# The MLP's second product turned to rows of tokens, 21 of its 32 groups computed with seven block products

## The chip, the cores and the metric

The kernel runs on one core of a Trainium2 chip. A core has TensorE (PE, with its weight loads shown apart as PEld), VectorE (DVE), ScalarE (ACT), GpSimd (POOL) and SyncE (SP), whose queue here issues nearly all DMAs. Each engine executes its own instructions in a fixed order and waits on semaphores for the others. The metric is the device time of one execution in microseconds (us). Before the change it was 2890.46 us, the median of three runs (2887.89 to 2895.62).

## The reference

One encoder layer over 2048 tokens of width 1024, in float32. The part that the change touches is the last one:

```python
h = h + xo @ w_xo[l]                         # after cross-attention
u = rmsnorm(h, norm_mlp_g[l]) @ w_up[l]      # 1024 -> 4096
h = h + jnp.square(jax.nn.relu(u)) @ w_down[l]   # 4096 -> 1024
return rmsnorm(h, norm_final_g)
```

Before it come a mixing layer (dilated sliding-window attention with three patterns, beside a width-31 convolution) and cross-attention to 256 memory tokens.

## The kernel before

**Numbers.** Every large product keeps float32 accuracy by splitting each operand in a high part (rounded by a cast) and a low part (the remainder). `mm3` (L198 to L201) then issues three matmuls: high by high, low by high, high by low. `wsplit2` (L187 to L192) makes the two parts of a weight tile: an ACT cast for the high part (L190), a subtraction for the low part (L191), on VectorE unless another engine is named.

**Stages.** A first part prepares the memory, the projections and the attention of the first tokens. Then four passes `post(p)`, p = 0 to 3, each take 512 tokens through the output projection (tiles `o`), cross-attention (`xs`, `x`), the MLP (`up`, `dn`) and the final norm. Beside the MLP of passes 0, 1 and 2 run the windowed attention and the convolution of the next 512 tokens: `weave` advances these generators by 0.95 and 0.6 of a step for each step of the pass. Pass 3 has nothing beside it. A scheduler then places every engine's instructions, so neighbouring steps interleave.

**The MLP of one pass.** The hidden 4096 features are cut in eight groups `fg` of 512. A group first makes its hidden values: four times 24 matmuls (`up`, 8 chunks of the contraction by 3), each into one of three PSUM banks; `rl` is max(0, up) times the norm's scale (VectorE, L1321), squared on ScalarE (L1322), and split in `hhh` (ACT, L1323) and `hhl` (VectorE, L1324). Then it multiplies by its 512 rows of `w_down`: for each of eight blocks of 128 output features, 12 matmuls (4 chunks by 3) with the weight as the stationary operand and 512 tokens as the moving one (`dn`), and VectorE adds the bank to `h` (L1339). `h` has features on partitions. After the last group `final` squares and sums over partitions, transposes each block of `h` by TensorE (`ot`, L1367), scales and stores.

**The feed of weights.** Each group loads eight tiles of 512 KB (four `raw_u`, four `raw_d`) through `wpost`: a DMA on SP into one of two `raw` buffers, ACT cast, VectorE subtraction, into one of four pairs `whi`/`wlo`. A `raw` buffer is free again after its subtraction, a pair after its last matmul. Each tile serves 24 matmuls.

**GpSimd** serves the attention beside the MLP: casts of queries (L821), the merging of the attention patterns (L914 to L939) and low parts in the convolution's norm (L272).

## Time and profile before

| | us |
|---|---|
| median of three runs | 2890.46 |
| the profiled execution | 2888.26 |
| its span, first to last instruction | 2886.5 |
| PE busy in the span | 2826.6 |
| VectorE busy | 1857.6 |
| ScalarE busy | 1166.3 |
| GpSimd busy | 458.0 |
| mean granted TensorE clock | 0.994 |

In the span, pass 0's MLP runs from 892 to 1287 us, pass 1's from 1442 to 1834, pass 2's from 1989 to 2380, and pass 3's from 2521 to the end. A row of groups reads: line, engine, operation, output<-inputs, shape and count, then busy time and mean duration of one, then the engine's idle time before these instructions and what ended it. A row of windows reads: the stretch, its length, busy time and count for PE, PEld, DVE, ACT and POOL, then the granted clock, the DMA engines' share and GB/s. Matmuls overlap one another, so the spacing of matmuls, and not the mean duration in a row, is what one of them costs.

### The profile page before, as it was taken

The numbers are of one execution on the slowest core, as the hardware profiler recorded it, in microseconds if no ns is written. First come the engines' busy times: TensorE is split into PE (matmuls) and PEld (weight loads), VectorE is DVE, ScalarE is ACT, GpSimd is POOL, SyncE is SP. The second block draws the span as 40 slices with busy tenths as digits, with TensorE's granted clock in tenths as the row PEclk, the third lists the DMA queues.
The fourth block names the chain that finished last, engine by engine and source line by source line (L and its number), as shares of the span: only waits on it lengthen the run. The fifth ranks groups of instructions, "written<-read, shape, count | busy, mean of one in ns | idle before, by whom it ended". The sixth has DMA issues, their size and how long they took to land.

```text
span 2886.5 us, 41313 instructions
## 1 busy us (share of the span) xinstructions
PE 2826.6 (98%) x15628; PEld 2376.2 (82%) x15628; DVE 1857.6 (64%) x3306; ACT 1166.3 (40%) x1988; POOL 458.0 (16%) x469
## 2 busy tenths in 40 slices
PE   8999999998999999999999999999999999999999
PEld 7878899887788888888888888888888888888887
DVE  5636535565789776557887765689876555544445
ACT  5633211475554333434543343444333433432233
POOL 1336421122102011200012012002011200000000
PEclk9999999999999999999999999999999999999999
DMA  8979845799734444554444446534543445333332
GB/s 264 295 173 228 202 132 131 182 256 247 205 102 131 135 133 123 168 160 145 121 130 130 138 117 192 175 96 128 142 127 109 139 132 175 93 90 101 96 95 74
DMA packets 598632, 433.74 MB, mean 150 GB/s; under 512 B 191550, under 2 KB 524786, under 8 KB 597921
## 3 DMA queue, kind: packets, MB, share of 16 engines
q1 hardware_dynamic: 558256, 408.21, 50.2%
q10 hardware_dynamic: 37952, 16.88, 2.4%
q0 software_dynamic: 2224, 6.01, 0.6%
q8 instruction: 123, 2.02, 0.3%
q14 instruction: 77, 0.62, 0.1%
HBM read 339.89 MB, written 91.11 MB: 149 GB/s over the span
## 4 chain that ended last, share of the span: by engine, by line
PE 82%; DVE 9%; DMA 5%; issue 2%; ACT 2%; POOL 1%; SPq 1%; POOLq 0%; DVEq 0%; ACTq 0%
PE dn L199 8%; PE dn L200 8%; PE dn L201 8%; PE up L199 7%; PE up L200 7%; PE up L201 7%; PE lin L199 4%; PE lin L201 4%; PE lin L200 4%; DVE cacc L216 3%; PE o L199 2%; PE o L200 2%; PE o L201 2%; PE xs L199 2%; PE xs L201 2%; PE xs L200 2%
## 5 line engine op out<-in xcount | busy, mean ns | idle before, releaser
L199 PE MATMUL dn<-hhh,whi_d 128*128 128x512 f32 (+1 forms) x1056 | 402.8, 392 | 7.2 <-DVE h L1339 6.1
L200 PE MATMUL dn<-hhl,whi_d 128*128 128x512 f32 (+1 forms) x1056 | 403.4, 385 | 1.1 <-DVE hhl L1324 1.1
L199 PE MATMUL up<-mh,whi_u 128*128 128x512 f32 x1024 | 402.9, 393 | 0.5 <-DVE rl L1321 0.5
L201 PE MATMUL dn<-hhh,wlo_d 128*128 128x512 f32 (+1 forms) x1056 | 402.6, 384 | 0.0
L200 PE MATMUL up<-ml,whi_u 128*128 128x512 f32 x1024 | 399.4, 390 | 1.0 <-DVE ml L1214 0.9
L201 PE MATMUL up<-mh,wlo_u 128*128 128x512 f32 x1024 | 399.7, 391 | 0.0
L216 DVE SCALAR_TENSOR_TENSOR cacc<-cu,cw,cacc 128x512 f32<-128x512 f32 x480 | 389.0, 811 | 5.5
L190 ACT CAST whi_d<-raw_d 128x1024 fp32r<-128x1024 f32 x128 | 134.6, 1052 | 418.1 <-PE up L200 378.6
L1339 DVE TENSOR_TENSOR h<-h,dn 128x512 f32<-128x512 f32 (+1 forms) x264 | 172.3, 667 | 162.9 <-PE dn L201 161.7
L190 ACT CAST whi_u<-raw_u 128x1024 fp32r<-128x1024 f32 x128 | 134.4, 1050 | 327.2 <-PE dn L200 304.1
L1321 DVE SCALAR_TENSOR_TENSOR rl<-up,ssumx 128x512 f32<-128x512 f32 x128 | 88.0, 690 | 256.9 <-PE up L201 252.6
L199 PEld LDWEIGHTS dn<-hhh,whi_d 128*128 128x128 f32 x1056 | 198.1, 189 | 47.5 <-DVE h L1339 10.2
L201 PEld LDWEIGHTS dn<-hhh,wlo_d 128*128 128x128 f32 x1056 | 198.8, 188 | 39.7
L200 PEld LDWEIGHTS dn<-hhl,whi_d 128*128 128x128 f32 x1056 | 199.3, 189 | 37.4 <-DVE hhl L1324 2.0
L200 PEld LDWEIGHTS up<-ml,whi_u 128*128 128x128 f32 x1024 | 192.4, 188 | 40.1 <-DVE ml L1214 2.3
L201 PEld LDWEIGHTS up<-mh,wlo_u 128*128 128x128 f32 x1024 | 192.2, 188 | 40.3
L199 PEld LDWEIGHTS up<-mh,whi_u 128*128 128x128 f32 x1024 | 192.4, 188 | 38.5 <-DVE rl L1321 0.9
L774 ACT ACTIVATE sm<-sm,o 128x256 f32<-128x256 f32 (+1 forms) x384 | 160.1, 466 | 126.3 <-DVE o L773 125.9
L773 DVE CUSTOM_DVE_ANT_0 sm<-s,mask 128x256 f32<-128x256 f32 (+1 forms) x384 | 128.5, 375 | 83.5 <-PE s L999 39.4
L191 DVE TENSOR_TENSOR wlo_u<-raw_u,whi_u 128x1024 fp32r<-128x1024 f32 x128 | 158.4, 1237 | 32.7 <-ACT whi_u L190 32.4
L191 DVE TENSOR_TENSOR wlo_d<-raw_d,whi_d 128x1024 fp32r<-128x1024 f32 x128 | 163.2, 1275 | 23.8 <-ACT whi_d L190 23.7
L177 POOL TENSOR_TENSOR nr<-st_v,mhalf 128x4 f32<-128x4 f32 (+1 forms) x13 | 13.0, 997 | 839.2 <-DVE st_v L173 839.2
(403 smaller groups left out, 6320.9 us busy)
## 6 DMA issues: line engine op xcount, KB each, us to landing
raw_u<-in_w_up_dram SPq DMA_DIRECT2D x128, 512.0 KB
raw_d<-in_w_down_dram SPq DMA_DIRECT2D x128, 512.0 KB
raw_o<-in_w_out_dram SPq DMA_DIRECT2D x32, 512.0 KB
raw_a<-ascr SPq DMA_DIRECT2D x32, 512.0 KB
raw_b<-bscr SPq DMA_DIRECT2D x32, 512.0 KB
k<-kscr SPq DMA_DIRECT2D x24, 512.0 KB
k<-kscr SPq DMA_DIRECT2D x8, 1152.0 KB
xn<-in_x_dram SPq DMA_DIRECT2D x32, 256.0 KB
```

The source lines that it names most:

```text
L177: POOL.tensor_tensor(dst, v, mhalf.to_broadcast([P, v.shape[1]]), op=ALU.pow)
L190: ACT.copy(hi, raw)
L191: (lo_eng or DVE).tensor_tensor(lo, raw, f(hi), op=ALU.subtract)
L199: PE.matmul(o, lh, rh, start=first, stop=False)
L200: PE.matmul(o, lh, rl, start=False, stop=False)
L201: last["pe"] = PE.matmul(o, ll, rh, start=False, stop=end)
L216: DVE.scalar_tensor_tensor(acc, u[:, t:t + 512], cw[:, c, t:t + 1], acc, op0=ALU.mult, op1=ALU.add)
L773: last["dve"] = DVE.tensor_tensor_reduce(dst, so, mask[:, 256 * m:256 * m + nk], 1.0, 3e38, ALU.add, ALU.min, mn)
L774: last["act"] = ACT.activation(dst, dst, AF.Exp, bias=mn, scale=-1.0)
L1321: last["dve"] = DVE.scalar_tensor_tensor(r, pt, 0.0, rsb, op0=ALU.max, op1=ALU.mult)
L1339: last["dve"] = DVE.tensor_tensor(hs[m][:, sl], hs[m][:, sl], pt, op=ALU.add)
```

## The change

The second product is computed with tokens on the output's partitions: the hidden values become the stationary operand (128 tokens at a time) and 512 columns of `w_down` the moving one. The running sum is kept in `rows` tiles (128 tokens by 512 features). It starts as `h`, transposed by TensorE in the middle of group 0's first product (`to_rows`: 32 transposes and 8 ACT copies a pass), and `final` now works on rows: squares with a sum along the row on ScalarE, one scaling instruction on VectorE for 128 tokens, a store of 512 KB, with no transposes.

In passes 1 to 3, groups 0 to 6 (21 of the 32) use Winograd's form of Strassen's algorithm (`seven`): tokens, hidden features and output features are each cut in two, and seven products of 12 matmuls replace eight. The sums of hidden values (S1 to S4) are built each time, by GpSimd and VectorE (`parts`), and split like the plain ones. The sums of weights are built once, in pass 0, by GpSimd (`sums_of`: four subtractions of 128x256 for each of 28 tiles), written to `dscr` in DRAM by 112 DMAs of 128 KB on SP, and read again in passes 1 to 3. Such a group loads seven tiles of `w_down` kind (three direct, four from `dscr`), each serving 12 matmuls; the low parts of five of the seven are made by GpSimd, of two by VectorE. The running products share PSUM: one pair of banks is added to the rows four times, with further matmuls accumulated between (`more`), another twice, the third once, which makes 14 additions a group in place of 8. Group 7 of each pass, and all of pass 0, keep eight products (`plain`).

The up and down products now rotate over four PSUM banks; the attention beside them has one score bank in place of two during the MLP. The activations' buffers become five interchangeable units of two tiles (`unit`), whose roles rotate from pass to pass.

```diff
@@ -117,6 +117,7 @@
+    dscr = dr.tile([7, 4, P, 2, 512], F32, name="dscr")
@@ -195,10 +196,11 @@
-    def mm3(o, lh, ll, rh, rl, first, end):
-        PE.matmul(o, lh, rh, start=first, stop=False)
-        PE.matmul(o, lh, rl, start=False, stop=False)
-        last["pe"] = PE.matmul(o, ll, rh, start=False, stop=end)
+    def mm3(o, lh, ll, rh, rl, first, end, more=False):
+        PE.matmul(o, lh, rh, start=first, stop=False, skip_group_check=more)
+        PE.matmul(o, lh, rl, start=False, stop=False, skip_group_check=more)
+        last["pe"] = PE.matmul(o, ll, rh, start=False, stop=end, skip_group_check=more)
@@ -1140,20 +1142,19 @@
-    xp_ = pool("post_x")
-    zp = pool("post_z")
-    yp = pool("post_y")
+    un = pool("post_u")
+    role = {x: i for i, x in enumerate("abcde")}
+    def unit(x, name, dtype=F32R):
+        return [un.tile([P, 4, 512], dtype, tag=f"un{role[x]}{i}", name=f"{name}{i}") for i in range(2)]
...
     def load_cat(p, half):
         d = cats.setdefault(p, {})
+        t = unit("ab"[half], f"cat{p}{half}")
         for q in "hl":
-            t = xquad(q, half, f"cat{q}{p}{half}")
             for e in range(4):
-                d[q, 4 * (1 - half) + e] = t[:, e]
+                d[q, 4 * (1 - half) + e] = t["hl".index(q)][:, e]
         for j in range(2):
             load_pair(p, half, j)
...
-        hs = [zp.tile([P, 512], F32, tag=f"z{m}", name=f"h{p}_{m}") for m in range(KC)]
-
-        def ytiles(name):
-            return {(q, k): ytile(q, k, f"{name}{q}{p}_{k}") for k in range(KC) for q in "hl"}
+        else:
+            banks["S"] = (3, 4)
+        he = unit("e", f"h{p}", F32)
+        hs = [he[m // 4][:, m % 4] for m in range(KC)]
+        yt = {q: unit(x, f"y{q}{p}") for q, x in zip("hl", "cd")}
+        y = {(q, k): yt[q][k // 4][:, k % 4] for k in range(KC) for q in "hl"}
...
@@ -1306,80 +1307,204 @@
-        for fg in range(FG):
-            hh = {}
...
+        banks["S"] = (4,)
+        acc = unit("b", f"rows{p}", F32)
+        def row(g, n=1):
+            r = acc[g // 4][:, g % 4:g % 4 + n]
+            return r if n > 1 else r[:, 0]
+        def to_rows(g):
+            t, c = divmod(g, 2)
+            pt = ps("T", f"hT{p}{g}")
+            for i in range(4):
+                PE.transpose(pt[:, P * i:P * i + P], hs[4 * c + i][:, P * t:P * t + P], ident)
+            ACT.copy(row(g), pt)
+        def add_rows(g, pt):
+            last["dve"] = DVE.tensor_tensor(row(g), row(g), pt, op=ALU.add)
+        def split(t, src):
+            ACT.copy(t[0], src)
+            DVE.tensor_tensor(t[1], src, f(t[0]), op=ALU.subtract)
+        def hidden(fg, c, up):
+            wh, wl = wpost(wcols(w_up, fg * 512 + c * P), f"u{p}{fg}_{c}")
+            pt = ps(up, "up")
+            for k in range(KC):
+                mm3(pt, wh[:, k, :], wl[:, k, :], y["h", k], y["l", k], k == 0, k == KC - 1)
+                if fg == 0 and k in ((1, 4) if c == 3 else (3, 7)):
+                    g = 2 * c + (k > 3)
+                    to_rows(2 * (g % 4) + g // 4)
+            r = tmp("rl")
+            last["dve"] = DVE.scalar_tensor_tensor(r, pt, 0.0, rsb, op0=ALU.max, op1=ALU.mult)
+            ACT.activation(r, r, AF.Square)
+            return r
+        def plain(fg, banks_, dn):
+            hh = unit("e" if fg == FG - 1 else "a", f"hh{p}{fg}")
-                wh, wl = wpost(wcols(w_up, fg * 512 + c * P), f"u{p}{fg}_{c}")
-                pt = ps("mm", "up")
...
-                last["dve"] = DVE.scalar_tensor_tensor(r, pt, 0.0, rsb, op0=ALU.max, op1=ALU.mult)
-                ACT.activation(r, r, AF.Square)
-                ACT.copy(hh["h", c], r)
-                DVE.tensor_tensor(hh["l", c], r, f(hh["h", c]), op=ALU.subtract)
+                r = hidden(fg, c, banks_)
+                split([t[:, c] for t in hh], r)
                 yield
             if fg == FG - 1:
-                fsum = ssum_tile(f"f{p}")
                 if not end:
                     load_cat(p + 1, 0)
-            def down(mp2, t, w, wh, wl):
...
+                gr = un.tile([P, 4, 512], F32, tag=f"un{role['d']}0", name=f"gain{p}")
+                gain_row[0] = gr[:, 0:2]
+                dma(gain_row[0].rearrange("p a m -> p (a m)"), A["norm_final_g"].unsqueeze(0).to_broadcast([P, D]))
+                if end:
...
+                        final(2 * th, 2)
...
+            for c in range(2):
+                pts = [ps(dn, "dn") for _ in range(4)]
+                for j in range(2):
+                    raw = wp.tile([P, 2, 2, 256], F32, tag="raw", name=f"raw_d{p}{fg}{c}{j}", bufs=2)
+                    for z in range(2):
+                        dma(raw[:, z], w_down.rearrange("(k p) (h m) -> p k h m", p=P, h=2)
+                            [:, 4 * fg + 2 * z + j, :, 256 * c:256 * c + 256])
+                    n = turn_w[0]
+                    turn_w[0] += 1
+                    wh, wl = wsplit2(wq if n % 4 > 1 else wp, raw, f"d{p}{fg}_{c}{j}", shape=(P, 2, 2, 256))
+                    if p == 0 and fg < FG - 1:
+                        sums_of(fg, c, j, raw)
+                    for t in range(4):
+                        for z in range(2):
+                            mm3(pts[t], *(x[:, 2 * z + j, P * t:P * t + P] for x in hh),
+                                *(x[:, z].rearrange("p h m -> p (h m)") for x in (wh, wl)), j + z == 0, j + z == 2)
+                        if j:
+                            a = row(2 * t, 2)[:, :, 256 * c:256 * c + 256]
+                            last["dve"] = DVE.tensor_tensor(a, a, pts[t].rearrange("p (h m) -> p h m", h=2), op=ALU.add)
+                    yield
+        def sums_of(fg, c, j, raw):
+            n = turn_s[0] % 2
+            turn_s[0] += 1
+            t = wsum[0][:, 2 * n:2 * n + 2].rearrange("p a (s m) -> p (a s) m", s=2)
+            for i, (a, b) in enumerate(((raw[:, 0, 1], raw[:, 0, 0]), (raw[:, 1, 1], t[:, 0]),
+                                        (raw[:, 1, 1], raw[:, 0, 1]), (raw[:, 1, 0], t[:, 1]))):
+                POOL.tensor_tensor(t[:, i], a, b, op=ALU.subtract)
+            for i in range(4):
+                dma(dscr[fg, i, :, j, 256 * c:256 * c + 256], t[:, i])
+        def seven(fg, up):
+            dx, dy = ("ux", "uy") if up == "up" else ("uy", "ux")
+            q = hq
+            A1, S3 = ([x[0][:, s].rearrange("p (j t) -> p j t", j=2) for x in q] for s in (0, 1))
+            A2, S12 = [x[0][:, 2:4] for x in q], [x[1][:, 0:2] for x in q]
+            S4 = [x[1][:, 2].rearrange("p (j t) -> p j t", j=2) for x in q]
+            rs_ = []
+            def parts(c):
+                r, j = rs_[c], c % 2
+                lo, hi = r[:, 0:256], r[:, 256:512]
+                if c < 2:
+                    split([x[:, j] for x in A1], lo)
+                    POOL.tensor_tensor(lo, lo, hi, op=ALU.subtract)
+                    split([x[:, j] for x in S3], lo)
+                else:
+                    r0 = rs_[j]
+                    W = DVE if j else POOL
+                    split([x[:, j] for x in A2], r)
+                    W.tensor_tensor(r0[:, 0:256], hi, r0[:, 0:256], op=ALU.subtract)
+                    W.tensor_tensor(r0[:, 256:512], r0[:, 256:512], hi, op=ALU.add)
+                    split([x[:, j] for x in S12], r0)
+                    W.tensor_tensor(lo, lo, r0[:, 0:256], op=ALU.subtract)
+                    split([x[:, j] for x in S4], lo)
+            for c in range(4):
+                rs_.append(hidden(fg, c, up))
+                for x in ((c - 1, c) if c % 2 else ()) if fg == 0 else (c,):
+                    parts(x)
                 yield
-        def final(t, w):
-            r = rstd_from(fsum[:, t:t + w])
...
-                    dma(out[0, 512 * p + c0:512 * p + c0 + P, 512 * g:512 * (g + 1)], ot)
+            def direct(a, b):
+            half = {"A11": A1, "S3": S3, "S4": S4, "A12": [x[:, :, lo] for x in A2], "A22": [x[:, :, hi] for x in A2],
+                    "S2": [x[:, :, lo] for x in S12], "S1": [x[:, :, hi] for x in S12]}
+            X, Y = ([ps(kind, "dn") for _ in range(2)] for kind in (dx, dy))
+            Z = None
+            for n, (key, w, out_, more, t0, c0) in enumerate((
+                    ("A11", direct(0, 0), 0, False, 0, 0), ("A12", direct(1, 0), 1, False, 0, 0),
+                    ("S2", dscr[fg, 1], 0, True, 0, 1), ("S1", dscr[fg, 0], 2, False, 2, 1),
+                    ("S3", dscr[fg, 2], 0, True, 2, 1), ("S4", direct(1, 1), 2, True, 0, 1),
+                    ("A22", dscr[fg, 3], 0, True, 2, 0))):
+                raw = wp.tile([P, 2, 512], F32, tag="raw", name=f"raw_d{p}{fg}{n}", bufs=2)
+                dma(raw, w)
+                wh, wl = wsplit2(wq if tw % 4 > 1 else wp, raw, f"d{p}{fg}_{n}", shape=(P, 2, 512),
+                                 lo_eng=None if n in (0, 4) else POOL)
+                if out_ == 2 and Z is None:
+                    Z = [ps(dy, "dn") for _ in range(2)]
+                pts = (X, Y, Z)[out_]
+                order_ = [(t, j) for j in range(2) for t in range(2)] if n in (1, 2) else \
+                    [(t, j) for t in range(2) for j in range(2)]
+                for t, j in order_:
+                    mm3(pts[t], *(x[:, j, P * t:P * t + P] for x in half[key]), wh[:, j], wl[:, j],
+                        not more and j == 0, j == 1, more)
+                    if j:
+                        add_rows(2 * (t0 + t) + c0, pts[t])
+                if n % 2 or n == 6:
+                    yield
+        fin = top.tile([P, 8], F32, tag="fin", name=f"fin{p}")
+        def final(t0, n):
+            for g in range(2 * t0, 2 * t0 + 2 * n):
+                ACT.activation(tmp("sq"), row(g), AF.Square, accum_out=fin[:, g:g + 1])
+            fv = fin[:, 2 * t0:2 * t0 + 2 * n].rearrange("p (t c) -> p t c", c=2)
+            sq = top.tile([P, 4], F32, tag="fsq", name="fsq")
+            DVE.tensor_tensor(sq[:, 0:n], fv[:, :, 0], fv[:, :, 1], op=ALU.add)
+            r = top.tile([P, 8], F32, tag="nr", name="nr", bufs=2)
+            rstd_col(r[:, 0:n], sq[:, 0:n], n, top)
+            for t in range(n):
+                x = row(2 * (t0 + t), 2)
+                DVE.scalar_tensor_tensor(x, x, r[:, t:t + 1], gain_row[0], op0=ALU.mult, op1=ALU.mult)
+                dma(out[0, 512 * p + P * (t0 + t):512 * p + P * (t0 + t + 1), :], x.rearrange("p a m -> p (a m)"))
+        banks.update(up=(0, 1, 2, 3), pu=(2, 3, 0, 1), ux=(0, 1), uy=(2, 3), q=(0, 1, 2, 3))
+        turn_s, wsum, hq = [0], [None], []
+        for k in ("up", "pu", "ux", "uy", "q"):
...
+        for fg in range(FG):
+            if fg == 0 and p:
+                hq += [unit("a", f"hh{p}"), unit("e", f"hl{p}")]
+            elif fg == 0:
+                wsum[0] = unit("e", "wsum", F32)[0]
+            if p == 0 or fg == FG - 1:
+                yield from plain(fg, *(("q", "q") if p == 0 else ("pu", "pu")))
+            else:
+                yield from seven(fg, ("up", "pu")[fg % 2])
+            if fg == FG - 1 and not end:
+                role.update(zip("abcde", [role[x] for x in "acdeb"]))
+                load_cat(p + 1, 1)
+        if not end:
+            final(0, 4)
+            for _ in range(4):
```

76 lines of the change are left out of this document (21 added, 55 removed).

## The prediction

> **What bounds the kernel now.** I read the page's first and fourth parts, then windows over the MLP's groups, then groups of instructions by shape inside one pass.
>
> ```profile
> span 2886.5 us, 41313 instructions
> PE 2826.6 (98%) x15628; PEld 2376.2 (82%) x15628; DVE 1857.6 (64%) x3306; ACT 1166.3 (40%) x1988; POOL 458.0 (16%) x469
> PE 82%; DVE 9%; DMA 5%; issue 2%; ACT 2%; POOL 1%; SPq 1%; POOLq 0%; DVEq 0%; ACTq 0%
> PE dn L199 8%; PE dn L200 8%; PE dn L201 8%; PE up L199 7%; PE up L200 7%; PE up L201 7%; PE lin L199 4%; PE lin L201 4%; PE lin L200 4%; DVE cacc L216 3%; PE o L199 2%; PE o L200 2%; PE o L201 2%; PE xs L199 2%; PE xs L201 2%; PE xs L200 2%
> ```
>
> TensorE carries 82% of the chain that ends last, and the two MLP products are 45% of it (24 for `dn`, 21 for `up`). So a matmul removed there is worth its spacing, as long as the other engines follow. Whether they do is read by stage. The rows are: groups 0 to 3 of passes 0, 1 and 2 (of pass 1 also group 0 alone, and groups 4 to 6); one group of pass 3; the time after the last product.
>
> ```profile
> 892.40:1098.90 206.50, 202.93 (x1103) 167.18 (x1102) 166.64 (x274) 77.27 (x124) 33.83 (x33) 0.99 0.47 133
> 1442.40:1645.60 203.20, 200.94 (x1103) 166.20 (x1102) 164.33 (x274) 77.09 (x124) 32.37 (x33) 1.00 0.48 133
> 1442.40:1495.30 52.90, 51.94 (x290) 42.68 (x289) 47.33 (x81) 21.08 (x35) 14.10 (x15) 1.00 0.47 135
> 1645.60:1789.70 144.10, 143.88 (x739) 119.17 (x739) 85.81 (x137) 59.36 (x87) 32.47 (x33) 1.00 0.50 144
> 1988.80:2193.60 204.80, 201.30 (x1100) 165.96 (x1099) 166.38 (x274) 76.95 (x124) 33.82 (x33) 1.00 0.47 131
> 2566.60:2610.20 43.60, 43.60 (x193) 35.91 (x192) 20.41 (x24) 13.04 (x16) 0.00 (x0) 1.00 0.33 96
> 2876.10:2886.50 10.40, 3.44 (x22) 2.48 (x21) 3.58 (x10) 1.79 (x3) 0.70 (x1) 0.75 0.34 132
> ```
>
> PE is never idle for long. VectorE is busy 81% of groups 0 to 3 of pass 1 (164.3 of 203.2), where attention and convolution run beside the MLP, 60% in groups 4 to 6, and 47% in pass 3 (20.4 of 43.6). GpSimd has room everywhere.
>
> **The matmuls removed.** A group of 192 matmuls takes 43.6 us in pass 3: 0.2271 us each at a granted clock of 1.00. A seven-product group has 84 matmuls for 96, so 12 x 0.2271 = 2.73 us less; 21 groups give 57.2 us. The 32 transposes of each pass move from its end into group 0: 0.
>
> **VectorE's part.** Rows of VectorE in pass 1, then in pass 3, then GpSimd, ScalarE, and `cacc` over the whole run (minimum/median/maximum, ns):
>
> ```profile
> L216 DVE SCALAR_TENSOR_TENSOR cacc<-cu,cw,cacc 128x512 f32<-128x512 f32 x78 | 61.2, 785 | 0.7
> L1339 DVE TENSOR_TENSOR h<-h,dn 128x512 f32<-128x512 f32 x63 | 42.1, 681 | 24.0 <-PE dn L201 23.7
> L191 DVE TENSOR_TENSOR wlo_d<-raw_d,whi_d 128x1024 fp32r<-128x1024 f32 x32 | 41.3, 1290 | 5.1 <-ACT whi_d L190 5.1
> L191 DVE TENSOR_TENSOR wlo_u<-raw_u,whi_u 128x1024 fp32r<-128x1024 f32 x30 | 37.5, 1250 | 12.0 <-ACT whi_u L190 11.9
> L1324 DVE TENSOR_TENSOR hhl<-rl,hhh 128x512 fp32r<-128x512 f32 x32 | 24.0, 753 | 0.8 <-ACT hhh L1323 0.5
> ```
> ```profile
> L191 DVE TENSOR_TENSOR wlo_d<-raw_d,whi_d 128x1024 fp32r<-128x1024 f32 x32 | 39.2, 1225 | 11.2 <-ACT whi_d L190 11.2
> L191 DVE TENSOR_TENSOR wlo_u<-raw_u,whi_u 128x1024 fp32r<-128x1024 f32 x29 | 35.5, 1224 | 3.8 <-ACT whi_u L190 3.8
> L1324 DVE TENSOR_TENSOR hhl<-rl,hhh 128x512 fp32r<-128x512 f32 x32 | 22.1, 692 | 0.2 <-ACT hhh L1323 0.2
> L1339 DVE TENSOR_TENSOR h<-h,dn 128x256 f32<-128x256 f32 x6 | 2.3, 419 | 1.2 <-PE dn L201 1.1
> ```
> ```profile
> L191 POOL TENSOR_TENSOR wlo_g<-raw_g,whi_g 128x1024 fp32r<-128x1024 f32 x8 | 19.1, 2394 | 13.9 <-ACT whi_g L190 13.9
> L821 POOL CAST qt<-qh 128x512 fp32r<-128x512 f32 x24 | 29.2, 1217 | 603.3 <-PE s L999 555.5 <-DMA ld<-oscr 47.8
> L529 POOL TENSOR_TENSOR vsq<-vsq 128x256 f32<-128x256 f32 x4 | 3.3, 823 | 0.2
> L190 ACT CAST whi_d<-raw_d 128x1024 fp32r<-128x1024 f32 x128 | 134.6, 1052 | 418.1 <-PE up L200 378.6 <-issue 23.1 <-DMA raw_d<-in_w_down_dram 13.0
> L216 DVE SCALAR_TENSOR_TENSOR cacc<-cu,cw,cacc x480: 698/748/2764, 239.5 to 2186.1; 128x512 f32<-128x512 f32 x160
> ```
>
> Per seven-product group: two `wlo_d` fewer, -2.5 us; 14 additions for 8, +6 x 0.68 = 4.1; the low parts of the hidden values are four of 512 and six of 256 columns for four of 512, +6 x 0.42 = 2.5; three sums of 256 on VectorE, 1.3. Together +5.4 us. GpSimd gains five subtractions of 1024 (12.0) and five of 256 (4.1): 16.1 us, with 8 us of its own in 51, so it isn't full. ScalarE gains three casts (3.2) and narrower splits; at 77 of 203 us it has the room.
>
> GpSimd's work also slows VectorE. Operations with both inputs in SBUF are longer in pass 1 than in pass 3: 32 x 0.065 (`wlo_d`) + 30 x 0.026 + 32 x 0.061 (`hhl`) + 78 x 0.037 (`cacc` against its median) = 7.8 us, for 64.8 us of GpSimd (32.4 and 32.5 in the two rows of windows): 0.12 us for each. This is the low end. At the high end such an operation waits for the whole GpSimd operation it meets (the longest `cacc` took 2.76 us), and with about half of VectorE's time in such operations that is 0.5. I take 0.2, nearer to the measured end, but above it because a 2.39 us subtraction meets more than one operation: 3.2 us a group.
>
> Groups 0 to 3 of pass 1 then ask 164.3 + 4 x (5.4 + 3.2) = 198.7 us of VectorE. PE would need 203.2 - 4 x 2.73 = 192.3. Filled to at most 96%, VectorE takes 207, some 15 us more than PE. A lag of about 5 us can be carried on, since tiles are made ahead, and is worked off in groups 4 to 6 (85.8 + 3 x 8.6 = 112 of 136 us). So PE waits about 10 us in each of passes 1 and 2: 20 in all. That is, the gain of these eight groups (21.8 us) is nearly lost.
>
> **Short waits.** A bank pair is accumulated on again 2.73 us after its last matmul, and between VectorE must add it (0.68 us); before, three banks gave 5.4 us. While PE waits there, the attention's matmuls wait behind. Bounds are 0 (pass 3 now has no idle time) and one addition at each of three reuses, 2.1 us a group. I take 0.6 in pass 3 (VectorE then 28.5 of 40.9 us) and 0.7 in groups 4 to 6: 4 + 4 us. The single score bank is freed by two VectorE operations of 256 columns (0.42) and used again two steps of 24 matmuls later, some 11 us: 0, at most 3.
>
> **Feed.** A load issued at 2563.67 us moves nothing for 1 us, 238 GB/s x 2.2 us (its 512 KB), then nothing:
>
> ```profile
> 2563.67 16.69 SPq L57 DMA_DIRECT2D raw_d<-in_w_down_dram  x4
> ...
> 2563.70:2564.70 1.00, 1.00 (x6) 0.84 (x5) 0.42 (x1) 0.00 (x0) 0.00 (x0) 1.00 0.00 0
> 2564.70:2566.90 2.20, 2.20 (x11) 1.81 (x11) 0.27 (x1) 0.13 (x1) 0.00 (x0) 1.00 0.74 238
> 2566.90:2569.10 2.20, 2.20 (x12) 1.81 (x11) 1.92 (x2) 0.92 (x1) 0.00 (x0) 1.00 0.00 0
> ```
>
> A `raw` buffer's turn is 3.2 + 1.05 + 2.39 + some 0.35 between engines = 7.0 us with GpSimd, 5.8 with VectorE. Eleven tiles over two buffers: (5 x 7.0 + 6 x 5.8) / 2 = 35 us a group, against 40.9 of PE. It is hidden, with 1.0 us to spare a turn (7.4 less 6.4). If GpSimd is late, the next load on SP is late, and with it the loads queued behind. I take 0 beyond the waits above.
>
> **Pass 0.** 112 subtractions by 0.82 us are 92 us of GpSimd, 13 a group, and their 112 stores (14.7 MB) pass through SP ahead of later loads. A `raw` buffer is then held for four subtractions (3.3 us), a turn of 7.8 us where two tiles last 10.9: hidden. VectorE loses 13 x 0.2 = 2.6 us a group, which matters only where it is fullest: +2 us, between 0 and 6.
>
> **The end.** After the last product now 10.4 us. Then: an addition 0.7, a square about as long, the root with GpSimd (0.70) and small steps some 1.9, two scalings of 1024 columns by 1.23, a store of 512 KB 3.2, an estimate of 9 to 9.5: -1, between -3 and +2.
>
> **Sum.** -57.2 + 20 + 4 + 4 + 2 - 1 = -28. Against the profiled execution (2888.26 us) that is 2860; the median shown is 2.2 us above it: about 2863 us.
>
> **The rivals.** *All hidden.* If VectorE keeps up (collisions at 0.12, lag carried), 10 us of waits remain: 2890 - 57 + 5 = 2838. For it: in group 0 of pass 1 VectorE was busy 47.3 of 52.9 us (89%) and PE idle only 1.0. Against it: 198.7 us do not fit in 192.3.
>
> *GpSimd shuts VectorE out* (the slower side). At 0.5 for each microsecond, 8 us a group: groups 0 to 3 ask 164.3 + 4 x 13.4 = 218, at 96% 227, less 192.3 and 5: 30 us in each of two passes. Groups 4 to 6, now 126 of 136 us full, lose 2 each (12), pass 3 1 a group (7), pass 0 4: -57 + 60 + 12 + 7 + 4 = +26, 2916 us. It decides from about 0.4, where the loss passes 57. The longest `cacc` speaks for it, the mean of 0.12 against it. The Trainium skill, page "SBUF — State Buffer", section Terms, says that VectorE and GpSimd share a port pair taken by lock for a whole instruction, so that "the loser **fully blocks**"; by that rule this rival is the case, and the `hhl` row (753 against 692 ns) shows only that operations met seldom so far.
>
> *The feed binds.* If a GpSimd subtraction waits in its queue behind attention work, so that a turn takes 8.4 us for 6.4, a group needs 46 us. This costs 5 us in pass 3 and in groups 5 and 6 of passes 1 and 2 (11 groups, 55 us), nothing where PE needs 47 anyway: 2890 - 57 + 55 = 2888, no change. The `qt` casts, each after some 23 us of waiting for PE (555.5 over 24), speak for it; the 1 us to spare speaks against it.
>
> **Chances.** Likeliest 0.45, its own range 2848 to 2882 (collisions 0.12 to 0.35); all hidden 0.15; shut out 0.20; feed 0.15; others, slower, 0.05. No change means within 0.3%, 2881.8 to 2899.1, about what a measurement of this kernel can tell. Faster: 0.43 + 0.15 + 0.04 of the feed's = 0.62; same: 0.02 + 0.09 = 0.11; slower: 0.20 + 0.02 + 0.05 = 0.27. The range 2836 to 2916 runs from all hidden to shut out and leaves out under 2 in 10.
>
> **What would show it.** Right: 84 `dn` matmuls in each of 21 groups; pass 3's groups at 41 to 42 us; groups 0 to 3 of passes 1 and 2 no shorter than 200 us, VectorE over 93% busy there, PE's waits on additions, `rl` and low parts. Shut out: `wlo_u` and `hl` much longer than 1.22 and 0.69 us wherever GpSimd is busy. Feed: PE waiting for `wlo_d` made by GpSimd, casts waiting for DMAs, in pass 3 too. The prediction fails if pass 3's groups aren't shorter, or if passes 1 and 2 gain as much as pass 3.

## The result and the profile after

The changed kernel takes 3010.97 us (median of four runs, 3009.01 to 3016.3), the kernel before beside it 2890.93: a ratio of 1.0416, with a 95% interval of 1.0402 to 1.043. It is 120 us slower, where the prediction had 2863 us and a range up to 2916. The profiled execution took 3009.49 us, with a span of 3007.7.

First the page of the changed kernel: its span, busy times, and the chain of work that ended last, by engine and by line.

```profile
span 3007.7 us, 41954 instructions
...
PE 2834.0 (94%) x15248; PEld 2338.4 (78%) x15248; DVE 2061.6 (69%) x3501; ACT 1283.2 (43%) x2217; POOL 918.2 (31%) x791
...
PE 55%; DVE 18%; DMA 12%; issue 5%; POOL 5%; ACT 3%; SPq 1%; POOLq 0%; DVEq 0%; ACTq 0%
```

TensorE's share of the chain has fallen from 82 to 55%; VectorE's has doubled, and DMA and GpSimd have more than doubled. GpSimd's busy time has doubled too (458 to 918 us). TensorE issues fewer matmuls and is busy a little longer.

Windows by stage (the stretch, its length, then the busy time of PE, PEld, DVE, ACT and POOL with their counts, the granted clock, the DMA share, GB/s): groups 0 to 3 of pass 0, groups 0 to 3 and 4 to 7 of pass 1, groups 0 to 3 of pass 2, and groups 1 to 6 of pass 3.

```profile
907.10:1124.60 217.50, 209.12 (x1134) 171.67 (x1134) 175.57 (x270) 80.56 (x131) 98.93 (x97) 0.98 0.55 160
1478.20:1723.80 245.60, 215.74 (x1128) 171.61 (x1126) 215.31 (x334) 104.69 (x172) 104.67 (x73) 0.92 0.47 134
1723.80:1920.50 196.70, 183.62 (x839) 146.63 (x839) 127.96 (x176) 87.15 (x127) 76.28 (x61) 0.97 0.58 171
2073.20:2315.90 242.70, 210.86 (x1128) 167.67 (x1126) 217.09 (x332) 103.95 (x172) 106.16 (x73) 0.94 0.46 133
2690.90:2953.20 262.30, 252.51 (x1081) 201.22 (x1080) 171.75 (x223) 110.25 (x151) 96.77 (x60) 1.00 0.43 132
```

Groups 0 to 3 of pass 1 take 245.6 us where they took 203.2; VectorE is busy 215.3 us of these (88%), and TensorE is idle 30 us. In pass 3 six groups take 262.3 us, 43.7 each, as before: with 12 matmuls less in each group, TensorE is now idle 10 us there, though VectorE is busy only 65% of the time and GpSimd 37%.

The time of each stage, from the first `up` matmul of a pass to the next pass's first `o` matmul (us, profiled executions):

| stage | before | after | difference |
|---|---|---|---|
| up to pass 0's MLP | 892.4 | 907.1 | +14.7 |
| MLP of pass 0 | 394.7 | 417.9 | +23.2 |
| MLP of pass 1 | 391.5 | 442.3 | +50.8 |
| MLP of pass 2 | 390.9 | 429.2 | +38.3 |
| MLP of pass 3 and the end | 365.8 | 368.0 | +2.2 |
| what lies between | 451.2 | 443.2 | -8.0 |

Groups of VectorE's instructions in the MLP of pass 1 (line, engine, operation, output and inputs, shape, count, then busy us, mean ns of one, idle time before them):

```profile
L218 DVE SCALAR_TENSOR_TENSOR cacc<-cu,cw,cacc 128x512 f32<-128x512 f32 x74 | 72.7, 984 | 0.5
L1326 DVE TENSOR_TENSOR rows<-rows,dn 128x512 f32<-128x512 f32 x98 | 64.4, 679 | 8.9 <-PE dn L203 8.8
L192 DVE TENSOR_TENSOR wlo_u<-raw_u,whi_u 128x1024 fp32r<-128x1024 f32 x30 | 37.9, 1262 | 33.5 <-ACT whi_u L191 32.7 <-POOL csm L927 0.7
L1331 DVE TENSOR_TENSOR hl<-rl,hh 128x256 fp32r<-128x256 f32 x42 | 35.1, 841 | 10.5 <-ACT hh L1330 10.0 <-PE hT L1322 0.5
L1331 DVE TENSOR_TENSOR hl<-rl,hh 128x512 fp32r<-128x512 f32 x28 | 29.6, 1059 | 7.1 <-ACT hh L1330 7.1
L192 DVE TENSOR_TENSOR wlo_d<-raw_d,whi_d 128x1024 fp32r<-128x1024 f32 x18 | 26.8, 1491 | 10.0 <-ACT whi_d L191 10.0
```

The operations that read both inputs from SBUF are stretched: `cacc` 984 ns (785 before), low parts of 512 hidden values 1059 (753 before), of 256 columns 841 (486 in a kernel without GpSimd work in the seven products, below), `wlo_d` 1491 (1290 before). `rows`, which adds a product out of PSUM, keeps its 679 ns (681 before). `wlo_u` is the exception: it reads both inputs from SBUF and hardly changes (1262, 1250 before).

### The profile page after: what moved, and what is told of

Same layout as the page of the kernel before. It is cut to its first block, busy times and chain, and to the rows that moved or that the text cites. A ratio compares the mean times of both kernels' runs of the same rounds, so it can differ in the third digit from the quotient of the medians.

```text
span 3007.7 us, 41954 instructions
## 1 busy us (share of the span) xinstructions
PE 2834.0 (94%) x15248; PEld 2338.4 (78%) x15248; DVE 2061.6 (69%) x3501; ACT 1283.2 (43%) x2217; POOL 918.2 (31%) x791
## 4 chain that ended last, share of the span: by engine, by line
PE 55%; DVE 18%; DMA 12%; issue 5%; POOL 5%; ACT 3%; SPq 1%; POOLq 0%; DVEq 0%; ACTq 0%
DVE cacc L218 4%; PE lin L201 4%; DMA raw_u<-in_w_up_dram 4%; PE lin L203 4%; PE lin L202 4%; PE dn L201 3%; DVE hl L1331 3%; PE up L202 3%; PE up L201 3%; PE up L203 3%; PE dn L202 3%; PE dn L203 3%; DMA raw_d<-in_w_down_dram 3%; PE o L202 2%; PE o L203 2%
## 5 line engine op out<-in xcount | busy, mean ns | idle before, releaser
L201 PE MATMUL dn<-whi_d,hh 128*128 128x512 f32 x940 | 390.3, 416 | 69.5 <-DVE rows L1326 41.0
L201 PE MATMUL up<-yh,whi_u 128*128 128x512 f32 x1024 | 404.5, 395 | 0.4 <-DVE h L1213 0.4
L202 PE MATMUL up<-yl,whi_u 128*128 128x512 f32 x1024 | 402.5, 393 | 0.5 <-DVE yl L1215 0.5
L203 PE MATMUL up<-yh,wlo_u 128*128 128x512 f32 x1024 | 400.9, 392 | 0.0
L202 PE MATMUL dn<-wlo_d,hh 128*128 128x512 f32 x940 | 377.8, 402 | 1.0 <-POOL wlo_d L192 1.0
L192 POOL TENSOR_TENSOR wlo_d<-raw_d,whi_d 128x1024 fp32r<-128x1024 f32 x105 | 258.9, 2467 | 222.2 <-ACT whi_d L191 221.9
L203 PE MATMUL dn<-whi_d,hl 128*128 128x512 f32 x588 | 229.7, 409 | 25.1 <-DVE hl L1331 24.5
L1326 DVE TENSOR_TENSOR rows<-rows,dn 128x512 f32<-128x512 f32 x302 | 197.3, 679 | 40.7 <-PE dn L203 40.4
L203 PEld LDWEIGHTS up<-yh,wlo_u 128*128 128x128 f32 x1024 | 192.9, 188 | 41.3
L202 PEld LDWEIGHTS up<-yl,whi_u 128*128 128x128 f32 x1024 | 193.0, 188 | 39.9 <-DVE yl L1215 1.4
```

The costliest lines, as they stand in the source:

```text
L192: (lo_eng or DVE).tensor_tensor(lo, raw, f(hi), op=ALU.subtract)
L201: PE.matmul(o, lh, rh, start=first, stop=False, skip_group_check=more)
L202: PE.matmul(o, lh, rl, start=False, stop=False, skip_group_check=more)
L203: last["pe"] = PE.matmul(o, ll, rh, start=False, stop=end, skip_group_check=more)
L1326: last["dve"] = DVE.tensor_tensor(row(g), row(g), pt, op=ALU.add)
```

## The experiments

"Over before" below is a median less the median of the kernel before in the same comparison (2888.6 to 2893.5 us), which takes out differences between chips. Stages are from the profiled executions.

### One pool or three

```diff
-    un = pool("post_u")
+    un = [pool("post_u"), pool("post_v"), pool("post_w")]
...
-        return [un.tile(
+        return [un[(0, 0, 1, 1, 2)[role[x]]].tile(
```

> The changed kernel with its five units in three pools (a and b, c and d, e) at the same addresses, nothing else. Theory: the first tile of a pool waits until everything that lay beneath the whole pool is done; in the changed kernel the loads of `cat` are issued at 731.8 us (704.8 before) and TensorE waits 13 us for them. Then the loads go back to about 705 us and the time is 2997 us (-14). If TensorE's +14.7 us ahead of pass 0's MLP have another cause, the time stays at 3011.

Measured 2996.86 us, +103.4 over before (the changed kernel: +120.0), so 17 us of the loss are gone. The timeline of SP's queue, before, after, and with three pools, at the first load of `cat`:

```profile
704.81 1.35 SPq L57 DMA_DIRECT2D cath<-cath  x2
```
```profile
731.79 0.57 SPq L57 DMA_DIRECT2D cat<-cath  x1
```
```profile
710.17 1.19 SPq L57 DMA_DIRECT2D cat<-cath  x2
```

In the changed kernel TensorE waits for these loads at the start of pass 0's `o` (its waits from 700 to 760 us):

```profile
PE o L201 <- DMA cat<-cath: 10.3, 1, 10.3
...
PE o L202 <- DMA cat<-catl: 2.6, 1, 2.6
```

With three pools these two waits are not there, and pass 0's MLP starts at 899 us in this run, and between 889 and 900 in the runs below that change nothing ahead of it (892 before, 907 in the changed kernel). So most of the 14.7 us ahead of pass 0's MLP comes from putting all units in one pool: the loads of the first two units were ordered 27 us later than before, with three pools 5 us. That this is because a pool's first tile waits for everything that lay beneath the whole pool was only argued; that the pool's cut decides it is shown. All experiments below have three pools.

### The form alone, the sums, and pass 3 alone

```diff
-            if p == 0 or fg == FG - 1:
+            if p >= 0 or fg == FG - 1:              # eight products everywhere; the sums left out
```

> With the three pools: rows of tokens in all 32 groups, eight block products everywhere, no sums of weights. What is left is the new form alone (transposes at the start, additions to rows, loads in other shapes, the single score bank, the end). If the form is neutral the time is that of the kernel before, 2888 to 2896; if the form itself costs what passes 0 to 3 lost, 2930 or more.

Measured 2883.54 us: -9.9 over before, ratio 0.9966 (0.9953 to 0.9979). Rows of tokens by themselves are a small gain, not a cost.

```diff
-            if p == 0 or fg == FG - 1:
+            if p >= 0 or fg == FG - 1:              # eight products everywhere; the sums kept
```

> As the kernel with rows of tokens alone, and GpSimd builds and stores the sums of weights in pass 0, which nothing reads. If GpSimd's 92 us of subtractions and their stores are what pass 0 lost, some 20 us more than without them; if pass 0 lost through the form (buffers held, banks), the same as without them.

Measured 2908.49 us, +15.0 over before: the sums cost 25 us, and pass 0's MLP takes 418.2 us against 392.2 without them. TensorE's waits in that stage:

```profile
PE dn L201 <- DVE rows L1394: 8.3, 3, 4.8
PE catT L949 <- POOL cat L941: 7.0, 1, 7.0
```

One wait of 7 us is for attention's merge on GpSimd, whose instructions stand in GpSimd's queue among sums that wait for their weights (83.5 us of waiting for these loads in pass 0).

```diff
-            if p == 0 or fg == FG - 1:
+            if p < NG - 1 or fg == FG - 1:          # seven products in pass 3 alone
```

> As the one with the sums, and pass 3 alone in seven products: 84 matmuls less, 19 us by their spacing. If the engines only hold each other up beside attention, this is 12 to 19 us faster than the sums alone; if the seven products bring their own waits (pass 3 showed no gain in the changed kernel), it is the same within 5 us, and so TensorE waits there for VectorE and GpSimd although both have room.

Measured 2907.76 us, +14.3 over before: no gain from 84 matmuls less, with no attention beside them. Windows over groups 1 to 6 of pass 3, first with eight products, then with seven:

```profile
2563.50:2827.40 263.90, 263.90 (x1154) 216.13 (x1153) 122.23 (x145) 78.21 (x96) 0.00 (x0) 1.00 0.32 96
```
```profile
2590.60:2853.00 262.40, 252.68 (x1082) 201.25 (x1081) 171.44 (x223) 110.31 (x151) 96.22 (x60) 1.00 0.44 132
```

262.4 for 263.9 us: 72 matmuls are gone, some 16 us. TensorE is idle for 9.7 us of that. Another 5 are lost around these waits and in stalls too short to be listed: of the spacings of matmuls in this stretch, 37 are longer than 0.26 us, and all others are 0.23 us, as with eight products. In the changed kernel's pass 3 (same stretch) the list of waits names the hand-offs:

```profile
POOL rl L1421 <- DVE hl L1331: 88.7, 11, 17.6
...
ACT hh L1330 <- POOL rl L1421: 23.8, 12, 2.4
ACT hh L1330 <- POOL rl L1428: 18.0, 6, 3.0
...
PE dn L201 <- DVE rows L1326: 9.8, 12, 1.3
```

The split of the last sums goes from engine to engine (GpSimd or VectorE subtracts, ScalarE casts, VectorE takes the low part), and VectorE's additions to `rows` stand in its queue behind it. TensorE waits for them 12 times in six groups, 9.8 us in all, to have its bank back.

With the first run, these make a ladder of the 120 us: the form -9.9, the sums +24.9, seven products in pass 3 -0.7, seven products in passes 1 and 2 +89.1, one pool +16.6. By the intervals of the runs a step is known to some 6 us.

### What GpSimd's part costs

Four edits of the 2996.86 us kernel. First, the low parts of all weights on VectorE:

```diff
-                                 lo_eng=None if n in (0, 4) else POOL)
+                                 lo_eng=None)
```

> The changed kernel with the three pools, and all seven low parts of a group's weights made by VectorE: GpSimd loses 5 subtractions of 1024 a group (12.0 of its 16.1 us), VectorE gains 5 x 1.23 = 6.1 us. If GpSimd's lateness and its collisions with VectorE are what passes 1 and 2 lost (89 us more than with eight products), VectorE asks 164 + 4 x 11.5 = 210 us in groups 0 to 3, filled to 96% 219 us, where now 268 are taken: some 40 us less in each of two passes, about 2915 us. If VectorE is the bound by its own load, it is slower than the 2997 us of the three pools by 20 us or more.

Measured 2928.51 us, +37.6 over before: 66 us of the loss are gone, though VectorE has more to do. In pass 3 the groups come down to 41.2 us. Next, the subtractions of hidden values on VectorE, the low parts left on GpSimd:

```diff
-                    POOL.tensor_tensor(lo, lo, hi, op=ALU.subtract)
+                    DVE.tensor_tensor(lo, lo, hi, op=ALU.subtract)
...
-                    W = DVE if j else POOL
+                    W = DVE
```

> With the three pools, and all eight subtractions of hidden values made by VectorE, the low parts of the weights left on GpSimd: GpSimd loses 4.1 of 16.1 us a group and nothing on it waits for VectorE's low parts any more; VectorE gains 5 x 0.41 = 2.1 us. If GpSimd's queue is held by subtractions that wait for VectorE (and so the weights' low parts, the raw buffers, the loads and the casts are late), most of the 89 us goes: 2920 to 2940 us. If the collisions at the port are the cause, a quarter of them goes with a quarter of GpSimd's work: 2975 to 2997 us.

Measured 2962.63 us, +71.7: between the two values expected, 32 us better for a quarter of GpSimd's work. Pass 3's groups take 41.6 to 42.8 us. Both edits together:

> With the three pools, and no GpSimd work in the seven products: low parts and subtractions all on VectorE. VectorE asks 164 + 4 x 8.7 = 199 us in groups 0 to 3 of passes 1 and 2; if it can be filled to 96% they take 207 to 210 us and the whole 2895 to 2910 us, close to the 2908 us of eight products with the sums. If VectorE's load itself is the bound (filled to 85% as in the changed kernel), 234 us and some 2950 us.

Measured 2928.16 us, +37.3: no better than the low parts alone, and 18 us above the range expected for a VectorE filled to 96%. (This expectation counted 8.7 us a group for VectorE. With eleven low parts of weights for eight it is 13.6: +3.7 for these, 4.1, 2.5 and 3.3 for the rest.) Windows over groups 0 to 3 and 4 to 7 of pass 1, and groups 1 to 6 of pass 3:

```profile
1463.10:1693.30 230.20, 211.42 (x1167) 169.91 (x1165) 208.09 (x375) 105.93 (x176) 33.72 (x35) 0.96 0.49 143
1693.30:1877.00 183.70, 176.55 (x799) 141.59 (x800) 137.58 (x205) 86.32 (x124) 29.02 (x29) 1.00 0.60 182
2629.20:2876.60 247.40, 247.40 (x1081) 202.62 (x1080) 192.20 (x284) 110.66 (x151) 0.00 (x0) 1.00 0.44 141
```

In pass 3 TensorE is never idle again: 41.2 us a group for 44.0 with eight products, 2.8 us less. In groups 0 to 3 of pass 1 VectorE is busy 90% of 230 us and holds 44% of the chain that ended last there; loads of weights hold 14% of it (none of its 18 longest entries with eight products). The fourth edit takes away one wait of GpSimd for VectorE:

```diff
-                    POOL.tensor_tensor(lo, lo, hi, op=ALU.subtract)
-                    split([x[:, j] for x in S3], lo)
+                    s = pp.tile([P, 256], F32, tag="s3", name="s3", bufs=1)
+                    POOL.tensor_tensor(s, lo, hi, op=ALU.subtract)
+                    split([x[:, j] for x in S3], s)
```

> With the three pools, and GpSimd's first subtraction (A11 - A12 halves of the hidden values) written to a tile of its own, so that it waits for the squared values alone and not for VectorE's low part of what it would overwrite; all work stays where it is. If that wait holds GpSimd's queue (34.6 us of waiting in 178 us of pass 1), 2940 to 2975 us; if not, 2997 us.

In this kernel the later sums (S1, S2, S4) take A11 where they should take A11 - A12, as that tile is no longer overwritten; the amount of work is the same. Measured 2977.73 us, +86.8: some 17 us less, 3 us above the range expected. Pass 3's groups take 42.8 us. So the queue of GpSimd held by VectorE is a part of it, and not the large one.

### Collisions or lateness

If GpSimd costs through collisions, work of its own that nobody waits for must cost the same. To the kernel without GpSimd work in the seven products:

```diff
+                if n not in (0, 4):
+                    for i in range(4):
+                        POOL.tensor_tensor(dm, dm, dm, op=ALU.subtract)
```

> The kernel with no GpSimd work in the seven products (2928 us), and in each such group 20 subtractions of 256 columns on GpSimd on a tile of their own that nobody reads, where the five low parts were: some 14.6 us a group, as much as the changed kernel gives GpSimd, without a raw buffer, a cast or a matmul waiting for it. If collisions with VectorE (and with attention's own GpSimd work) are what GpSimd's part costs, 2970 to 2995 us. If it is the lateness of what GpSimd makes (low parts late, raw buffers late, loads and casts late), 2928 to 2940 us. In pass 3, where the groups take 41.2 us: 43 or more by collisions, 41 to 42 by lateness.

Measured 2987.69 us, +98.9, but it did not test this: with no operand to hold it, all of the idle work was ordered into the time around pass 0 (the answer for this line; its first and last start in us):

```profile
L1461 POOL TENSOR_TENSOR dm<-dm x420: 604/616/1670, 744.1 to 1323.8; 128x256 f32<-128x256 f32 x140
```

Passes 1 to 3 took 415.9, 410.8 and 351.8 us, as without it (413.9, 412.3, 351.7), and pass 0 455.9 for 417.0. Around pass 0 the idle work cost 57 us (17.9 ahead of its MLP, 38.9 in it), with VectorE busy 67.2 us longer for GpSimd's 347.1 (0.19 for each); how much of that is attention's own GpSimd work standing behind it, this run doesn't tell. So the second try takes the product's own weights as an operand:

```diff
-                        POOL.tensor_tensor(dm, dm, dm, op=ALU.subtract)
+                        POOL.tensor_tensor(dm, dm, f(wh[:, 0, 0:256]), op=ALU.subtract)
```

> The kernel with no GpSimd work in the seven products (2928 us), and 20 subtractions of 256 columns a group on GpSimd that nobody reads, this time taking the high part of the same product's weights as an operand, so that they run beside that product and not all in pass 0. No raw buffer, cast or matmul waits for them. If GpSimd's work costs by collisions with VectorE and by making attention's own GpSimd work late, 2960 to 2985 us (14.6 us a group at 0.2 to 0.4 us of VectorE each is 12 to 23 us in groups 0 to 3 of each of two passes). If it costs by the lateness of the low parts (raw buffers, loads, casts), 2928 to 2940 us. Pass 3's groups: 41.2 to 42 us either way, as VectorE has 9 us of room there; 43 or more would speak for collisions.

Measured 3006.14 us, +117.5 over before, 80 us more than without the idle work, and more than the changed kernel with three pools (+103.4). The same three stretches as above:

```profile
1461.20:1711.80 250.60, 218.98 (x1167) 174.21 (x1165) 235.08 (x373) 105.95 (x176) 118.05 (x115) 0.93 0.45 131
1711.80:1903.00 191.20, 180.58 (x800) 143.55 (x801) 151.53 (x205) 85.66 (x124) 91.03 (x89) 0.98 0.57 175
2693.40:2953.00 259.60, 253.44 (x1082) 200.94 (x1081) 221.16 (x283) 111.54 (x151) 126.76 (x120) 1.00 0.43 135
```

The counts on PE, VectorE and ScalarE are the same to within two instructions; only GpSimd has 80 more in the first stretch, and VectorE is busy 27.0 us longer for GpSimd's 84.3: 0.32 us for each. In the other two it is 0.23 (14.0 for 62.0, 29.0 for 126.8). VectorE's groups in the MLP of pass 1, first without the idle work, then with it:

```profile
L192 DVE TENSOR_TENSOR wlo_d<-raw_d,whi_d 128x1024 fp32r<-128x1024 f32 x53 | 66.4, 1254 | 9.6 <-ACT whi_d L191 9.5
L1326 DVE TENSOR_TENSOR rows<-rows,dn 128x512 f32<-128x512 f32 x98 | 64.0, 682 | 3.0 <-PE dn L203 3.0
L218 DVE SCALAR_TENSOR_TENSOR cacc<-cu,cw,cacc 128x512 f32<-128x512 f32 x74 | 56.9, 769 | 0.2
...
L1331 DVE TENSOR_TENSOR hl<-rl,hh 128x256 fp32r<-128x256 f32 x42 | 20.2, 486 | 2.9 <-ACT hh L1330 2.8
L1331 DVE TENSOR_TENSOR hl<-rl,hh 128x512 fp32r<-128x512 f32 x28 | 20.0, 721 | 0.0
```
```profile
L192 DVE TENSOR_TENSOR wlo_d<-raw_d,whi_d 128x1024 fp32r<-128x1024 f32 x53 | 72.6, 1370 | 9.3 <-ACT whi_d L191 9.3
L218 DVE SCALAR_TENSOR_TENSOR cacc<-cu,cw,cacc 128x512 f32<-128x512 f32 x74 | 64.4, 870 | 0.2
L1327 DVE TENSOR_TENSOR rows<-rows,dn 128x512 f32<-128x512 f32 x98 | 63.5, 677 | 1.9 <-PE dn L203 1.9
...
L1332 DVE TENSOR_TENSOR hl<-rl,hh 128x256 fp32r<-128x256 f32 x42 | 28.7, 688 | 3.9 <-ACT hh L1331 3.9
L1332 DVE TENSOR_TENSOR hl<-rl,hh 128x512 fp32r<-128x512 f32 x28 | 25.3, 911 | 0.0
```

The same operations grow (721 to 911, 486 to 688, 769 to 870, `wlo_d` 1254 to 1370 ns), and `rows`, with its one input in PSUM, does not. Little waits for this work. It does read a weight's high part and shares GpSimd's queue with attention, but in the whole run ScalarE waits 0.6 us for it and TensorE's weight loads 1.0 us, and TensorE waits less for attention's merge than without it (0.5 us in pass 1, for 2.5). So lateness isn't needed: collisions alone make a loss of the size seen (80 us, where the changed kernel's own work on GpSimd in the seven products costs 66: +103.4 with it, +37.3 without). That lateness adds nothing in the changed kernel is not shown by this.

The idle work is not the changed kernel's own: in pass 1 it took 147.9 us of GpSimd, where the changed kernel's low parts and subtractions took 120.2. So the rate is better read from the changed kernel itself, against the same rows without GpSimd work. `cacc` 74 x 0.215 us, `hl` 42 x 0.355 and 28 x 0.338, `wlo_d` 18 x 0.237 make 44.6 us in the MLP of pass 1, and 48.2 with all other rows that both kernels have, for 118.2 us more of GpSimd: 0.41. The same sum over groups 0 to 3 gives 34.2 for 71.0, which is 0.48, and over groups 1 to 6 of pass 3 24.2 for 96.8, which is 0.25. So there is no single rate: in each of the two kernels it is highest where VectorE is fullest, and in the changed kernel it is no lower than beside idle work.

Pass 3 is the surprise. There too the groups go from 41.2 to 43.3 us with VectorE busy 85%, where the expectation counted its room as cover: the stretched operations stand in the chain that hands the sums and the banks on, and TensorE waits for that chain (4.1 us for `hl`, 2.0 for `rows`; without the idle work it has no wait there).

### VectorE's load

```diff
         for t in range(1, CW):
-            DVE.scalar_tensor_tensor(acc, u[:, t:t + 512], cw[:, c, t:t + 1], acc, op0=ALU.mult, op1=ALU.add)
+            if n < 2:
+                DVE.scalar_tensor_tensor(acc, u[:, t:t + 512], cw[:, c, t:t + 1], acc, op0=ALU.mult, op1=ALU.add)
```

> The changed kernel with the three pools (2997 us), and all taps but the first of the convolution left out for the stretches of tokens that are made beside passes 1 and 2, so some 61 us of VectorE's work less in groups 0 to 3 of each (the output then lacks these taps). If VectorE's load is the bound there, these groups fall from 244 to 200 or 210 us in each pass: 2915 to 2930 us. If the engines hold each other up whatever the load, above 2960 us.

Measured 2930.96 us, +42.2: 61 us less than with the convolution, a microsecond above what was expected from VectorE's load. Groups 0 to 3 of pass 1, with the convolution and without:

```profile
1467.80:1711.60 243.80, 214.66 (x1128) 170.54 (x1126) 214.83 (x334) 104.48 (x172) 103.50 (x73) 0.91 0.47 135
1467.60:1681.80 214.20, 201.65 (x1094) 161.76 (x1092) 148.19 (x252) 102.01 (x168) 93.51 (x71) 0.98 0.50 149
```

They fall from 243.8 to 214.2 us. VectorE is then busy only 69%, and TensorE is still idle 12.6 us, where it was 29.1: VectorE is the larger part, and hand-offs such as those of pass 3 remain. The run doesn't part VectorE's load from collisions, since the taps that it leaves out (`cacc`) are themselves among the stretched operations.

### What the sums cost

```diff
-            for i in range(4):
-                dma(dscr[fg, i, :, j, 256 * c:256 * c + 256], t[:, i])
```

> Rows of tokens in all groups with the sums of weights built by GpSimd in pass 0 and not stored. If GpSimd's time and its waits for the weights are what the sums cost, 2908 us as with the stores (2884 without sums); if the 112 stores in SP's queue are, 2884 us.

Measured 2891.61 us, +2.8 over before, neither of the two values: of the 25 us of the sums, 12.7 come with GpSimd's work (the wait for attention's merge is 5.8 of them) and 12.2 with the stores. With the stores in place, SP's waits in pass 0 begin with:

```profile
SPq L57 <- POOL wsum L1403: 93.5, 84, 4.0
```

So a store holds SP's queue, and the loads behind it. To test that, they were issued on GpSimd's queue:

```diff
-                dma(dscr[fg, i, :, j, 256 * c:256 * c + 256], t[:, i])
+                dma(dscr[fg, i, :, j, 256 * c:256 * c + 256], t[:, i], nc.gpsimd)
```

> Rows of tokens in all groups, the sums of weights built in pass 0 and their 112 stores issued on GpSimd's queue, not SP's. SP waits 93.5 us in 84 waits for GpSimd's sums before it can issue a store, and the loads behind are late. If that order is what the stores cost (2908 us with, 2892 without them), 2890 to 2896 us; if the 14.7 MB of traffic are, 2908 us; if GpSimd pays for issuing them, more than 2908.

Measured 2909.12 us, +20.5: no gain, though SP's waits for the sums fell from 93.5 to 32.3 us. So the order in SP's queue isn't shown to be what the stores cost. Either the traffic is what they cost, or GpSimd pays for issuing them what SP no longer loses; this stays open.

### A version that beats both

Seven products in six groups of pass 3 alone, their low parts and subtractions on VectorE; the sums of two groups built in each of passes 0 to 2, in the fourth and sixth group of the pass (the order of the groups, `perm`, differs by pass so that six different ones come there):

```diff
-                    if p == 0 and fg < FG - 1:
+                    if not end and fg in (3, 5):
...
-            if p == 0 or fg == FG - 1:
+            if not end or fg in (0, FG - 1):
```

> Rows of tokens everywhere (2884 us without sums); seven products in six groups of pass 3 alone, all their work off GpSimd; the sums of the six groups built two in each of passes 0 to 2, in the fourth and sixth group of the pass, where the sums in pass 0 cost 0 to 3 us (the order of the groups is changed for it). If only the place of GpSimd's work matters: -6 x 2.8 = -17 and 0 to +6 for the sums: 2867 to 2873 us. If the sums cost 25 us for seven groups wherever they are: 2888 us.

Measured 2866.51 us, half a microsecond under the range expected and 22.3 us less than before: a ratio of 0.9928 (0.9911 to 0.9945), and 12 us less than eight products everywhere. The page, and windows over pass 0's MLP and groups 1 to 6 of pass 3:

```profile
PE 2816.5 (98%) x15428; PEld 2357.8 (82%) x15428; DVE 1914.8 (67%) x3366; ACT 1202.8 (42%) x2082; POOL 542.6 (19%) x565
```
```profile
896.60:1288.40 391.80, 391.67 (x2051) 324.00 (x2050) 270.26 (x417) 153.63 (x236) 92.53 (x96) 1.00 0.52 152
2566.50:2814.10 247.60, 247.60 (x1081) 202.68 (x1081) 190.56 (x282) 109.44 (x149) 0.00 (x0) 1.00 0.44 138
```

The sums are nearly hidden at these places (the MLP of passes 0 to 2 takes 391.8, 392.0 and 393.4 us, without them 392.2, 392.0 and 391.4), and six groups save 16.3 us (247.6 for 263.9). Against rows of tokens without sums, 12.4 of these are left, so the sums cost some 4 us. The run changes two things at once, the place of the sums and how many stand in one pass; which of them helps is not told apart.

## Why the prediction was wrong

The prediction's terms against the ladder, in us:

| term | predicted | measured |
|---|---|---|
| the form and the end | -1 | -9.9 |
| the sums in pass 0 | +2 | +24.9 |
| the units' pool | not seen | +16.6 |
| pass 3: 84 matmuls less, and short waits | -19 + 4 | -0.7 |
| passes 1 and 2: 168 matmuls less, and VectorE | -38 + 20 + 4 | +89.1 |

**The matmuls removed.** Right where nothing stands in the way: 2.8 us a group in pass 3 once GpSimd is out of it (forecast 2.73), 84 `dn` matmuls for 96.

**VectorE's part, the step that failed.** The bound was named rightly: VectorE in groups 0 to 3 of passes 1 and 2. Its price, 10 us of TensorE's waiting in each of the two passes, was wrong in two terms. Collisions were taken at 0.2 us for each of GpSimd's; in groups 0 to 3 of pass 1 of the changed kernel it was 0.48 (0.32 beside idle work). VectorE was taken to be fillable to 96%; it was 88% busy in the changed kernel, 90% without GpSimd's work and 94% with idle work. So 198.7 us of work in 207 became 215.3 us in 245.6, and TensorE was idle for 30 us. Of VectorE's own waits in these groups 10.1 us were for casts of weights, 7.9 for loads of attention and only 1.2 for casts of hidden values; the other 10 or so were for matmuls and small steps. Even with no collision added, the fuller VectorE costs time: without GpSimd work passes 1 and 2 still take 43 us more (413.9 + 412.3) than with eight products (392.0 + 391.0), where the sum allowed -14 with collisions. Of the 89.1 us that these passes lost, 43 are thus left without GpSimd's work, and some 46 come with it.

**Short waits.** 0.6 us a group was taken in pass 3, between 0 and 2.1. The end not taken came true, 1.6 us of waits (9.8 in six groups), and with the slower matmuls around them a group lost 2.5 us (43.7 for 41.2), which is outside the bound. The reason wasn't in the bound: VectorE's additions were priced alone, at 0.68 us, and not as the last link behind sums that pass through three engines in VectorE's queue.

**Feed.** 0 was taken, and this is not settled. No wait of TensorE in pass 3 is for a weight, and with all low parts on VectorE the same two buffers keep TensorE full there. But ScalarE waits 70.4 us for `raw_u` in pass 3 of the changed kernel, VectorE waits 29.4 for these casts, and the additions that TensorE waits for stand behind them: of the chain that ended last, loads of weights hold 20% in this stretch and 13% in groups 0 to 3 of pass 1. Beside the idle work of pass 3, where the low parts are VectorE's, no load is among the chain's 18 longest entries, and the groups are nearly as long (43.3 us). So late loads aren't needed for the loss, but in the changed kernel they are on its path, as the rival *the feed binds* had it; no run has a third `raw` buffer, which would part the two.

**Pass 0.** +2 was forecast on the ground that the buffers' turns are long enough. TensorE indeed waits for no weight there. What cost was attention's merge, which stood behind sums on GpSimd (7 us of TensorE's waiting), and the stores, 12 us; how the stores cost them stays open.

**The rivals.** *GpSimd shuts VectorE out* came nearest: collisions are shown by work that hardly anything waits for, and its rate of 0.5 is about what the changed kernel has where VectorE is fullest (0.48), though not in pass 3 (0.25). Its time of 2916 us was 95 short: it had +34 for passes 1 and 2 (-38 + 60 + 12) where 89.1 was measured, -12 for pass 3 where it was -0.7, 4 for pass 0 where it was 24.9, and nothing for the pool. Its threshold ("from about 0.4") was too high: with no GpSimd work in the seven products at all, passes 1 and 2 already lost 43 us. The Trainium skill, page "SBUF — State Buffer", section Who interferes with whom, says that a VectorE instruction with both inputs in SBUF contends with GpSimd instructions that read SBUF, and one with at most one such input, outside the 2-port modes, does not. The traces agree: `hl` 486 to 688 ns and 721 to 911, `rows` 682 and 677. That such an instruction need not be hit each time is seen in `wlo_u`, which stays at its length in pass 1 (1262 ns) and grows from 1314 to 1481 beside the idle work around pass 0. The prediction set the low mean before (0.12) against this rival, and said of the `hhl` row that it shows only that operations met seldom so far; the second reading was the better one.

**What would show it.** The test set ("fails if pass 3's groups aren't shorter") was the right one, and it failed: 43.7 us as before. The sign of VectorE over 93% busy failed too (88%). The signs of *shut out* came half: `hl` is much longer, `wlo_u` is not. Two sums of the prediction don't come out as written, without weight for the forecast: *all hidden* adds 5 us where it speaks of 10, and 20.4 and 8.6 us of VectorE a group make 29.0, not 28.5.

## What to carry to other kernels

A free engine is not free work: before giving GpSimd subtractions of SBUF tiles, count the VectorE operations with two SBUF inputs beside them and add 0.2 to 0.5 us for each microsecond of GpSimd (0.25 in pass 3 of this kernel, 0.48 where VectorE is fullest), also where VectorE has room, because its operations stand in chains. Where three engines pass each tile of a short product on, price the chain and the queue it stands in, not the busiest engine's share. Work ahead of time can be spread: the sums of weights of seven groups cost 25 us in one pass, those of six groups, two in each of three passes, some 4 us.
